# Forgetting attention on one Trainium2 core: the causal mask of diagonal blocks as a GpSimd select on the exponentials, in place of a third product in PSUM

## The chip, the cores and the metric

The kernel runs on one core of a Trainium2 chip. The core has five engines with queues of their own, each working strictly through its own program: TensorE (matmul; in the profile PE, and PEld for the loading of weights), VectorE (DVE), ScalarE (ACT), GpSimd (POOL) and SyncE (SP, which only issues transfers here). They wait for each other by semaphores. The metric is the device time of one execution in microseconds; of several runs the median counts.

## What is computed

One decoder layer with two groups of attention heads over a sequence of 2048. The edit is in the first group, forgetting attention: eight heads of width 64, causal, with a bias from cumulated log forget gates. Cut to what matters:

```python
def forgetting_attention(q, k, v, f_logit):
    cum = jnp.cumsum(jax.nn.log_sigmoid(f_logit.astype(jnp.float32)), axis=1)
    ...
    def one_block(args):
        qb, cb, n = args
        s = jnp.einsum('bhqd,bhkd->bhqk', qb, kh, preferred_element_type=jnp.float32) * scale
        s = s + cb[..., None] - cum[:, :, None, :]
        q_pos = n * Q_BLOCK + jnp.arange(Q_BLOCK)
        causal = key_pos[None, :] <= q_pos[:, None]
        s = jnp.where(causal, s, -jnp.inf)
        p = jax.nn.softmax(s, axis=-1)
        return jnp.einsum('bhqk,bhkd->bhqd', p.astype(vh.dtype), vh)
```

Around it: a normalised and modulated input, one input projection, a second group with a sliding window of 128 and sinks, SiLU gates, an output projection, a normalisation and the residual.

## The kernel before

The kernel works in float32 accuracy by splitting operands in a high and a low float16 part. It goes through three stretches: first setup, normalisation, projections and sliding-window attention; then the sweep of forgetting attention; then the output projection.

**The sweep.** It is a list of 160 steps, numbered from 0: eight heads of 20 steps. A head has four query chunks of 512 queries (`ci` = 0 to 3), and a chunk takes its key blocks of 128 in pairs, so 2, 4, 6 and 8 steps. Scores stand transposed: keys on the 128 partitions, queries along the row, at most 2 x 512 columns. The last two steps of a chunk hold the four diagonal blocks. There the columns of earlier queries are left out, so their widths are 512 + 384 = 896 and 256 + 128 = 384 columns instead of 1024. In a head these are the steps 0, 1, 4, 5, 10, 11, 18 and 19: 64 diagonal steps with 128 diagonal blocks in all.

**One step** has five parts, spread over its neighbours:

- `scores` (TensorE, line 1294 and 1295): per key block two products into the score tile `st` in PSUM (`sta` in the profile; there is only one such tile). The second product adds the cross terms, gate biases and row maxima. On a diagonal block a third (line 1297), an identity times `dmaskT`, adds -1e30 above the diagonal to the first 128 columns.
- `exp32` (ScalarE, line 1301): exponential of the tile to `p32`, float32, in SBUF (three buffers).
- `high` (ScalarE, line 1305): `p32` rounded to float16, the first half of `ph`.
- `low` (VectorE, line 1308): the rest, `p32` minus that half, to the second half of `ph`.
- `pv` (TensorE, lines 1318 to 1321): three small products for each 128 queries with the values.

The order of the work is written out by hand in the main loop. In step s, each engine's queue gets its share of this sequence: `exp32` of s; a `tick`, which releases delayed work such as the evacuation of projection tiles; `low` of s - 1; the first half of the step's filling work; `high` of s; `scores` of s + 1; a `tick`; `pv` of s - 2; the second half of the filling work. The filling work is projections of later heads (line 317) and products for row maxima of later chunks (line 1245, reduced by VectorE on lines 1248 and 1250).

So on ScalarE the copy `high` follows its exponential with only released evacuations between, and the exponential of the next step follows behind. On TensorE `scores` of s + 2 need the score tile that `exp32` of s + 1 reads out.

**GpSimd** does nothing in the sweep but issue transfers: gate tiles to memory (line 359, after VectorE's product on 357), weights (215), the maximum of a weight tile to memory and back (224, after VectorE's reduction on 221, and 229), and the output gate's weights (1176). In the setup it builds masks with `affine_select`, among them `dm32t` on line 514, which ScalarE turns into `dmaskT` (551); `identb` is a bfloat16 identity (458).

The row sum comes from a column of ones beside the values, so it holds what `ph` holds.

Of the kernel before, what the change touches and what calls it, by code (L numbers as in the profile page):

```python
# [10 lines left out]
F32 = mybir.dt.float32  # L11
F16 = mybir.dt.float16
BF16 = mybir.dt.bfloat16
I32 = mybir.dt.int32
AF = mybir.ActivationFunctionType
ALU = mybir.AluOpType
AX = mybir.AxisListType

P = 128
# [9 lines left out]
NEG = -1.0e30  # L29
# [4 lines left out]
XM, XR, VW = 66, 69, 129  # L34
# [7 lines left out]
def hybrid_layer(  # L42
# [17 lines left out]
    V, A, G, PE, SP = nc.vector, nc.scalar, nc.gpsimd, nc.tensor, nc.sync  # L60
# [12 lines left out]
    const = ctx.enter_context(tc.tile_pool(name="const", bufs=1))  # L73
# [73 lines left out]
    Shp = const.tile([P, KT], F32, name="Shp")  # L147

    ident = const.tile([P, P], F32, name="ident")
    identb = const.tile([P, P], BF16, name="identb")  # L150
    identh = const.tile([P, P], F16, name="identh")
    dmaskT = const.tile([P, P], BF16, name="dmaskT")
    lift = const.tile([P, 1], F32, name="lift")
    pfl = const.tile([P, 1], F32, name="pfl")
    csum = const.tile([P, 8, NB], F32, name="csum")
# [272 lines left out]
    start = ExitStack()  # L428
    st = start.enter_context(tc.tile_pool(name="start", bufs=1, reuse_waits="tile"))
    wad = start.enter_context(tc.tile_pool(name="wad", bufs=8, reuse_waits="tile"))  # L430
    with tc.manual_schedule():
# [23 lines left out]
            w_load(key, pieces(key))  # L455
        G.dma_start(snk[:], sinks[0].partition_broadcast(P))
        G.dma_start(bfg[:], b_fgate[0].partition_broadcast(P))
        V.tensor_copy(identb[:], ident[:])
        V.tensor_copy(identh[:], ident[:])
        PE.transpose(bk[0][:, :P], rows[:], ident[:])  # L460
        cols = st.tile([P, 40], F32, name="cols")
# [41 lines left out]
        zero = st.tile([P, 2 * P], F32, name="zero")  # L503
# [5 lines left out]
        dm32 = st.tile([P, P], F32, name="dm32")  # L509

        G.affine_select(dm32[:], zero[:, :P], [[-1, P]], ALU.is_ge, NEG, base=0, channel_multiplier=1)
        dm32t = st.tile([P, P], F32, name="dm32t")

        G.affine_select(dm32t[:], zero[:, :P], [[1, P]], ALU.is_ge, NEG, base=0, channel_multiplier=-1)

        G.affine_select(triu[:], ones[:], [[1, P]], ALU.is_ge, 0.0, base=0, channel_multiplier=-1)

        ang = st.tile([P, CH], F32, name="ang")
# [29 lines left out]
        A.activation(cs_[:], kh[:], AF.Sin)  # L548
        A.activation(sn_[:], sp_[:], AF.Copy, scale=-1.0)
        A.activation(dmask[:], dm32[:], AF.Copy)  # L550
        A.activation(dmaskT[:], dm32t[:], AF.Copy)

        def col8(name):
            return st.tile([P, KT], F32, name=name)
# [282 lines left out]
    class Pair:  # L837
# [9 lines left out]
        def scores(self):  # L847
            self.pss = ps_s.tile([P, 2, CH], F32, tag="s", name="pss")
            q = ab[self.j, self.i // 4]
            for e, (i, k0, nk) in enumerate(self.blocks):  # L850
                qo, o = (i % 4) * P, e * 2 * P
                for n, (a, b) in enumerate(((0, 0), (0, 1), (1, 0))):
                    for h in range(2):
                        r = slice(64 * h, 64 * h + 64)
                        PE.matmul(self.pss[:, h, o:o + nk * P], q[r, a, qo:qo + P],  # L855
                                  kst[self.g][r, b, k0 * P:(i + 1) * P], start=(n == 0), stop=(n == 2))
# [228 lines left out]
    with swa_order:  # L1085
# [10 lines left out]
        base = N_PRO  # L1096
# [179 lines left out]
    class Step:  # L1276
# [9 lines left out]
        def scores(self):  # L1286
            T, ci = Ts[self.hd % 2], self.ci
            self.st = ps_st.tile([P, 2 * CH], F32, tag="st", name="sta")
            for b, u0, o in self.blocks:
                w = CH - u0 * P  # L1290
                kb_ = slice(b * P, (b + 1) * P)
                qc = slice(ci * CH + u0 * P, (ci + 1) * CH)
                diag = b >= 4 * ci
                PE.matmul(self.st[:, o:o + w], T[:, 3, kb_], T[:, 1, qc], start=True, stop=False)  # L1294
                PE.matmul(self.st[:, o:o + w], T[0:XR, 2, kb_], T[0:XR, 0, qc], start=False, stop=not diag)  # L1295
                if diag:
                    PE.matmul(self.st[:, o:o + P], identb[:], dmaskT[:], start=False, stop=True)

        def exp32(self):
            self.p32 = fxp.tile([P, 2 * CH], F32, tag="p32", name="p32")  # L1300
            A.activation(self.p32[:, :self.w], self.st[:, :self.w], AF.Exp, scale=scl[f"qk{self.hd}"][:], bias=lift[:])  # L1301

        def high(self):
            self.ph = fxh.tile([P, 2, 2 * CH], F16, tag="ph", name="pha")
            A.activation(self.ph[:, 0, :self.w], self.p32[:, :self.w], AF.Copy)  # L1305
# [376 lines left out]
```

## Time and profile before

| | |
|---|---|
| median of 3 runs | 1194.2 us (1192.35 to 1195.01) |
| span of the profiled execution | 1188.7 us |
| TensorE busy in it | 1147.3 us (97%) |
| VectorE | 914.1 us (77%) |
| ScalarE | 665.9 us (56%) |
| GpSimd | 115.2 us (10%) |
| the sweep | about 480 to 1021 us |

The table's busy times are of one profiled execution; its span runs from its first to its last instruction. In rows of groups the columns are: line, engine, operation, output and inputs, shapes and count; then busy time in us and mean ns of one; then the engine's idle time just before, with what ended it. In rows in order of time the first number is the start in us, the second the duration, and brackets hold the idle time before it and its releaser. A row "A <- B" among the waits says how long A's engine stood idle until B was done: total, times, longest. Matmuls overlap in the array, so the time from one start to the next is their price, not their duration.

### The profile page before, as it was taken

What the parts mean: (1) busy time and instruction counts of PE and PEld (TensorE: products, weight loads), DVE (VectorE), ACT (ScalarE), POOL (GpSimd) and SP (SyncE); (2) the same over time, 40 slices, a digit from 0 to 9 for tenths busy, and PEclk for the clock granted to TensorE, in tenths of its full rate; (3) what the DMA queues carried; (4) which work ended last, traced back from release to release, by engine and by line L of the source; (5) the groups of instructions that cost most, each with busy time, mean ns of one, the idle gap of its engine ahead of it and who ended that gap; (6) DMA issues with size and microseconds to landing.
All of it is one profiled execution on the core that took longest, in us unless ns stands there. A gap on an engine that the chain in (4) does not pass through costs nothing.

```text
span 1188.7 us, 27244 instructions
## 1 busy us (share of the span) xinstructions
PE 1147.3 (97%) x10853; PEld 693.6 (58%) x10853; DVE 914.1 (77%) x2263; ACT 665.9 (56%) x1102; POOL 115.2 (10%) x231
## 2 busy tenths in 40 slices
PE   5899999999999998999999999999999999999997
PEld 2475556765558976555555555555555555555554
DVE  7876678687776748688888889887888887766665
ACT  2784345464655521476766667666666778433332
POOL 2000112212121211001000101001000000000000
PEclk9899999999999999999999999999999999999999
DMA  9745433314223322413325322212311345455642
GB/s 333 277 121 87 84 89 99 61 59 109 83 70 88 58 63 63 65 50 95 68 70 72 102 63 60 50 48 71 48 42 39 92 127 176 147 171 184 198 167 96
DMA packets 87579, 120.22 MB, mean 101 GB/s; under 512 B 27508, under 2 KB 63388, under 8 KB 87452
## 3 DMA queue, kind: packets, MB, share of 16 engines
q1 hardware_dynamic: 76184, 85.69, 24.4%
q0 software_dynamic: 10832, 32.50, 13.2%
q8 instruction: 85, 1.39, 0.6%
q14 instruction: 42, 0.34, 0.1%
q10 hardware_dynamic: 436, 0.28, 0.1%
HBM read 71.04 MB, written 25.18 MB: 81 GB/s over the span
## 4 chain that ended last, share of the span: by engine, by line
PE 79%; DVE 10%; DMA 6%; issue 2%; ACT 2%; SPq 1%; DVEq 0%; ACTq 0%
PE bk L317 29%; PE bk L1489 13%; PE bk L335 7%; PE sta L1295 4%; PE sta L1294 4%; PE bk L1245 4%; PE poa L1320 2%; PE poa L1321 2%; PE poa L1318 2%; DMA wa<-in_w_ada_dram 2%; PE pxb L888 2%; PE pss L855 2%; PE pob L907 2%; DVE a_m L1248 1%; PE bk L1410 1%
## 5 line engine op out<-in xcount | busy, mean ns | idle before, releaser
L1301 ACT ACTIVATE p<-sta,lift,scl_qk 128x1024 f32<-128x1024 f32 (+2 forms) x160 | 172.0, 1075 | 143.7 <-PE sta L1295 88.2
L317 PE MATMUL bk<-hT,wh_qk 128*128 128x512 f16 x768 | 195.3, 380 | 0.0
L1248 DVE TENSOR_REDUCE a_m<-bk 128x1 f32<-128x512 f32 x192 | 130.5, 686 | 55.2 <-PE bk L1245 54.0
L1308 DVE TENSOR_TENSOR pha<-p,pha 128x1024 f16<-128x1024 f32 (+2 forms) x160 | 169.1, 1057 | 0.2 <-ACT pha L1305 0.2
L1489 PE MATMUL bk<-wohl,oz 128*128 128x512 f16 x744 | 167.0, 379 | 0.7 <-DVE oz L1438 0.7
L1305 ACT ACTIVATE pha<-p 128x1024 f16<-128x1024 f32 (+2 forms) x160 | 148.1, 926 | 5.4 <-PE poa L1321 0.7
L1489 PEld LDWEIGHTS <-oz 128*128 128x128 f16 x744 | 71.9, 99 | 79.4 <-DVE oz L1438 2.8
L317 PEld LDWEIGHTS <-wh_qk 128*128 128x128 f16 x768 | 72.5, 98 | 78.2 <-issue 6.6
L1321 PE MATMUL poa<-vt,pha 128*128 128x65 f16 x1088 | 116.1, 192 | 1.4 <-DVE pha L1308 1.2
L1318 PE MATMUL poa<-vt,pha 128*128 128x65 f16 x1088 | 116.5, 193 | 0.5 <-DVE ona L1327 0.4
L1320 PE MATMUL poa<-vt,pha 128*128 128x64 f16 x1088 | 116.5, 194 | 0.0
L1245 PE MATMUL bk<-T 66*128 66x512 f16 (+2 forms) x320 | 110.2, 350 | 3.1 <-DVE a_m L1248 3.0
L1294 PE MATMUL sta<-T 128*128 128x512 f16 (+1 forms) x320 | 110.9, 346 | 2.5 <-ACT p L1301 2.4
L1318 PEld LDWEIGHTS <-pha 128*128 128x128 f16 x1088 | 101.5, 96 | 15.1 <-DVE ona L1327 1.5
L1295 PE MATMUL sta<-T 69*128 69x512 f16 (+1 forms) x320 | 109.8, 348 | 0.0
L1320 PEld LDWEIGHTS <-pha 128*128 128x128 f16 x1088 | 100.9, 97 | 11.4
L1321 PEld LDWEIGHTS <-pha 128*128 128x128 f16 x1088 | 100.8, 99 | 1.8 <-DVE pha L1308 1.7
L317 PE MATMUL bk<-hT,wh_za 128*128 128x512 f16 x384 | 99.7, 378 | 0.0
L335 PE MATMUL bk<-wh_va,hT 128*128 128x128 f16 x1536 | 90.7, 219 | 0.0
L335 PEld LDWEIGHTS <-hT 128*128 128x128 f16 x1536 | 87.5, 98 | 4.7 <-issue 2.1
L317 PE MATMUL bk<-hT,wh_zb 128*128 128x512 f16 x384 | 88.9, 379 | 0.0
L317 PE MATMUL bk<-hT,wh_qb 128*128 128x512 f16 x384 | 87.4, 379 | 0.0
(498 smaller groups left out, 1860.4 us busy)
## 6 DMA issues: line engine op xcount, KB each, us to landing
hT<-in_x_dram SPq DMA_DIRECT2D x20, 512.0 KB
wa<-in_w_ada_dram SPq DMA_DIRECT2D x16, 512.0 KB
z_d<-tz POOLq DMA_DIRECT2D x32, 256.0 KB, 2.9
T<-stq SPq DMA_DIRECT2D x64, 128.0 KB
T<-o_d SPq DMA_DIRECT2D x16, 512.0 KB
T<-z_d SPq DMA_DIRECT2D x16, 512.0 KB
out_dram<-hT SPq DMA_DIRECT2D x15, 512.0 KB
xt<-in_x_dram SPq DMA_DIRECT2D x12, 512.0 KB
```

The costliest lines, as they stand in the source:

```text
L317: PE.matmul(ps, whl[:, a, k, :], hT[ci][:, b, k, :], start=(k == 0 and n == 0), stop=(k == KT - 1 and n == 2))
L335: PE.matmul(ps[:, u * P:(u + 1) * P], hT[ci][:, a, k, u * P:(u + 1) * P], whl[:, b, k, :], start=(k == 0 and n == 0), stop=(k == KT - 1 an ...
L1245: PE.matmul(mx[:, :w], T[0:XM, 0, i * P:(i + 1) * P], T[0:XM, 2, pc * CH:pc * CH + w], start=True, stop=True)
L1294: PE.matmul(self.st[:, o:o + w], T[:, 3, kb_], T[:, 1, qc], start=True, stop=False)
L1295: PE.matmul(self.st[:, o:o + w], T[0:XR, 2, kb_], T[0:XR, 0, qc], start=False, stop=not diag)
L1301: A.activation(self.p32[:, :self.w], self.st[:, :self.w], AF.Exp, scale=scl[f"qk{self.hd}"][:], bias=lift[:])
L1305: A.activation(self.ph[:, 0, :self.w], self.p32[:, :self.w], AF.Copy)
L1308: V.tensor_tensor(self.ph[:, 1, :self.w], self.p32[:, :self.w], self.ph[:, 0, :self.w], op=ALU.subtract)
L1318: PE.matmul(po[:, u, :], ph[:, 0, pq], vt[:, b, hd, 0:65], start=(self.first and n == 0 and u == 0), stop=False)
L1320: PE.matmul(po[:, u, 0:64], ph[:, 0, pq], vt[:, b, hd, 65:VW], start=False, stop=False)
L1321: PE.matmul(po[:, u, :], ph[:, 1, pq], vt[:, b, hd, 0:65], start=False, stop=(self.last and n == len(self.blocks) - 1))
L1489: PE.matmul(py, self.hl[:, i, k, :], w_slot(8 * j + k)[:, cc], start=(k == 0 and m_ == 0), stop=(k == KT - 1 and m_ == 2))
```

## The change

The third product of the diagonal blocks goes, with the two constants that it reads. After the exponential of a diagonal step GpSimd sets to zero, in place in `p32`, what stands above the diagonal: the first 128 columns of each of the step's two blocks, which begin at column 0 and at `o1` (512 or 256). One instruction serves both; `[[0, 2], [1, P]]` counts the block with step 0 and the column with step 1, the partition with -1, so that a column is kept where query minus key is at least 0. `high` and `low` read `p32` after it.

```diff
-    identb = const.tile([P, P], BF16, name="identb")
...
-    dmaskT = const.tile([P, P], BF16, name="dmaskT")
...
-        V.tensor_copy(identb[:], ident[:])
...
-        dm32t = st.tile([P, P], F32, name="dm32t")
-
-        G.affine_select(dm32t[:], zero[:, :P], [[1, P]], ALU.is_ge, NEG, base=0, channel_multiplier=-1)
-
...
-        A.activation(dmaskT[:], dm32t[:], AF.Copy)
...
-                diag = b >= 4 * ci
                 PE.matmul(self.st[:, o:o + w], T[:, 3, kb_], T[:, 1, qc], start=True, stop=False)
-                PE.matmul(self.st[:, o:o + w], T[0:XR, 2, kb_], T[0:XR, 0, qc], start=False, stop=not diag)
-                if diag:
-                    PE.matmul(self.st[:, o:o + P], identb[:], dmaskT[:], start=False, stop=True)
+                PE.matmul(self.st[:, o:o + w], T[0:XR, 2, kb_], T[0:XR, 0, qc], start=False, stop=True)
 
         def exp32(self):
             self.p32 = fxp.tile([P, 2 * CH], F32, tag="p32", name="p32")
             A.activation(self.p32[:, :self.w], self.st[:, :self.w], AF.Exp, scale=scl[f"qk{self.hd}"][:], bias=lift[:])
+            if self.blocks[0][0] >= 4 * self.ci:
+
+                o1 = self.blocks[1][2]
+                dg = self.p32[:, :2 * o1].rearrange("p (b c) -> p b c", b=2)[:, :, 0:P]
+                G.affine_select(dg, dg, [[0, 2], [1, P]], ALU.is_ge, 0.0, base=0, channel_multiplier=-1)
```

## The prediction

> **What bounds the kernel now.** I read the page's head first, then the busy time by stretches, then who waited for whom, and at last single steps in order of time. The edit lies in the sweep of forgetting attention, which runs from about 480 to 1021 us.
>
> ```profile
> span 1188.7 us, 27244 instructions
> ...
> core 0: us, PE busy (x) PEld busy (x) DVE busy (x) ACT busy (x) POOL busy (x), PEclk, DMA share, GB/s
> 480.00:1021.00 541.00, 534.43 (x5496) 310.54 (x5495) 456.48 (x984) 372.88 (x440) 35.64 (x57) 1.00 0.32 73
> ```
>
> In this stretch TensorE is busy for 534.4 of 541 us at a granted clock of 1.00, VectorE for 456.5, ScalarE for 372.9, GpSimd for 35.6. A busy TensorE need not be a full one, since the ends of matmuls are modelled, so the waits are read beside it.
>
> ```profile
> PE sta L1294 <- ACT p L1301: 2.4, 5, 0.7
> PE bk L1245 <- DVE a_m L1248: 1.7, 4, 0.7
> ...
> ACT p L1301 <- PE sta L1295: 88.2, 74, 4.0
> ACT p L1301 <- PE sta L1297: 46.0, 41, 4.9
> ```
>
> Columns: waited in total, times, longest. In the whole sweep TensorE waited 2.4 us for the exponentials and 1.7 us for the maxima; the exponentials waited 134 us for TensorE (88.2 + 46.0). So TensorE sets the pace and ScalarE follows with slack. What shortens TensorE's stream here is worth its full length, until the slack of ScalarE is used up.
>
> **What is removed.** The third product of a diagonal block, line 1297.
>
> ```profile
> L1297 PE MATMUL sta<-dmaskT,identb 128*128 128x128 bf16 x128 | 26.5, 219 | 0.0
> ...
> 751.04 0.38 PE L1295 MATMUL sta<-T 69*128 69x512 f16 x1
> 751.26 0.22 PE L1297 MATMUL sta<-dmaskT,identb 128*128 128x128 bf16 x1
> 751.32 0.32 PE L1294 MATMUL sta<-T 128*128 128x384 f16 x1
> ...
> 751.65 0.22 PE L1297 MATMUL sta<-dmaskT,identb 128*128 128x128 bf16 x1
> 751.71 0.19 PE L1318 MATMUL poa<-vt,pha 128*128 128x65 f16 x1
> ```
>
> The first row gives the count, 128, and 26.5 us of busy time. That is not the price: 0.22 us is how long one is in flight, and the next product starts 0.06 us after it (751.26 to 751.32, 751.65 to 751.71). A quarter of the 512 columns that take 0.22 us from start to start (751.04 to 751.26) is 0.055. So 128 products give back 128 x 0.055 = 7.0 to 128 x 0.06 = 7.7 us; I take 7.4. Their weight loads run under other products and add nothing. The setup of the two constants goes away too: a cast and a select, of 0.23 and 0.29 us by the rows below, and a copy.
>
> ```profile
> L551 ACT ACTIVATE dmaskT<-dm32t 128x128 bf16<-128x128 f32 x1 | 0.3, 295 | 0.0
> ...
> PEld bk L479 <- DMA wa<-in_w_ada_dram: 6.0, 3, 4.1
> ```
>
> They stand in the first 20 us, on three engines, while TensorE's first products wait for weights from memory; I count them as nothing, and 0.3 us if that cover were gone.
>
> **What is added.** One GpSimd select in each of 64 diagonal steps (two per query chunk, four chunks, eight heads), on 2 x 128 columns in place. The trace has the operation in its setup, in the same size.
>
> ```profile
> 1.09 0.29 POOL masks.py:199 TENSOR_SCALAR_AFFINE_SELECT ident<-ident 128x128 f32<-128x128 f32 x1
> ...
> 1.41 0.23 DVE L458 CAST identb<-ident 128x128 bf16<-128x128 f32 x1 [0.19 <-POOL ident masks.py:199]
> ...
> 5.99 0.27 DVE L504 MEMSET zero<- 128x256 f32 x1
> ...
> 6.33 0.40 POOL L507 TENSOR_SCALAR_AFFINE_SELECT bm<-zero 128x256 f32<-128x256 f32 x1 [0.89 <-DVE zero L504]
> ```
>
> The select takes 0.40 us, starts 0.07 us after what it waited for (5.99 + 0.27 = 6.26 to 6.33), and a reader starts 0.03 us after its end (1.38 to 1.41). The new detour, from the end of the exponential to the earliest start of the float16 copy on line 1305, is so 0.5 us undisturbed; I use 0.6. The setup rows are selects on a quiet chip, so the other end stays open upwards and is priced below.
>
> Who waits for it: ScalarE, whose queue holds the copy and, behind it, the next step's exponential; behind that the scores of the step after next on TensorE, which need the score tile emptied. The row of an ordinary diagonal pair shows the cover.
>
> ```profile
> 500.22 1.10 ACT L1301 ACTIVATE p<-sta,lift,scl_qk 128x896 f32<-128x896 f32 x1 [1.72 <-PE sta L1297]
> 501.35 0.95 ACT L1305 ACTIVATE pha<-p 128x896 f16<-128x896 f32 x1
> 502.52 0.67 ACT L1301 ACTIVATE p<-sta,lift,scl_qk 128x384 f32<-128x384 f32 x1 [0.22 <-PE sta L1297]
> 503.31 0.52 ACT L1305 ACTIVATE pha<-p 128x384 f16<-128x384 f32 x1
> 505.70 1.20 ACT L1301 ACTIVATE p<-sta,lift,scl_qk 128x1024 f32<-128x1024 f32 x1 [1.86 <-PE sta L1295]
> ```
>
> Behind the wide copy ScalarE stood idle for 0.22 us, behind the narrow one for 1.86. A detour of 0.6 delays the second exponential (502.52 to 503.19) by about 0.4. Next on TensorE come the scores whose end released the third, at 505.70: four products of 0.22, so they began at about 504.7, and 0.4 late is still in time. The third isn't delayed at all. So an ordinary pair costs nothing; without that slack, 64 x 0.6 = 38 us would be the price.
>
> **GpSimd's queue.** The selects are put in among its DMA issues, in program order, and a select behind an issue that waits for VectorE starts late. This is the part that costs. Step 41 (second of head 2) in full:
>
> ```profile
> 625.88 0.67 ACT L1301 ACTIVATE p<-sta,lift,scl_qk 128x384 f32<-128x384 f32 x1 [1.61 <-PE sta L1297]
> 626.58 0.52 ACT L1305 ACTIVATE pha<-p 128x384 f16<-128x384 f32 x1
> 629.12 1.20 ACT L1301 ACTIVATE p<-sta,lift,scl_qk 128x1024 f32<-128x1024 f32 x1 [2.02 <-PE sta L1295]
> ...
> 627.51 0.57 POOL L224 DMA_DIRECT2D mx_d<-w_mx  x1 [21.98 <-DVE w_mx L221]
> 628.07 0.55 POOL L1176 DMA_DIRECT2D gw<-in_w_ada_dram  x1
> ...
> 628.06 1.08 DVE L1308 TENSOR_TENSOR pha<-p,pha 128x896 f16<-128x896 f32 x1
> ...
> 630.45 0.38 PE L1294 MATMUL sta<-T 128*128 128x512 f16 x1
> ```
>
> Both issues were put into the queue in step 40, ahead of the select of step 41. They are done at 628.62, so the copy starts at about 629.05 instead of 626.58 and ends at 629.6, the exponential of step 42 (629.12 to 630.32) ends 0.5 late, and the scores of step 43, which TensorE began at 630.45, are 0.3 to 0.4 us late. That is loss on the path.
>
> I did this for 62 diagonal steps (all but the last two, where no such scores follow): the copy starts at the later of exponential + detour and GpSimd's queue + 0.4, the ScalarE rows up to the next exponential are pushed, and what exceeds TensorE's start of the scores counts. With a detour of 0.6 the sum is 2.4 us, at five places: steps 20, 41, 81 and 145 behind an issue that waited for VectorE, and step 138 with 0.2. The first and the last of the four:
>
> ```profile
> 555.49 0.94 ACT L1305 ACTIVATE pha<-p 128x896 f16<-128x896 f32 x1
> ...
> 556.94 0.56 POOL L224 DMA_DIRECT2D mx_d<-w_mx  x1 [17.20 <-DVE w_mx L221]
> ...
> 970.24 0.52 ACT L1305 ACTIVATE pha<-p 128x384 f16<-128x384 f32 x1
> ...
> 971.39 0.54 POOL L359 DMA_DIRECT2D z_d<-tz  x1 [38.01 <-DVE tz L357]
> ```
>
> Each time GpSimd is free 1.7 to 2.0 us after the copy once began (557.5 against 555.49, 971.93 against 970.24). Longer detours sum to 2.9 us at 0.9, 3.7 at 1.2, 4.7 at 1.5, 6.8 at 1.8, 11.2 at 2.1 and 20.7 at 2.5: the slack gives way at about 1.8.
>
> The other way round, the issues behind a select now wait for that step's exponential, 1 to 3 us. They are loads of weights used many steps later and stores read after the sweep; GpSimd stood idle for 22 us ahead of the issue at 627.51. I count nothing.
>
> **VectorE.** Its subtraction of line 1308 reads the float32 tile and the copy, both in SBUF, and takes 1.08 us in the row above. If a select can't run beside it, a select that comes late into one waits for its rest: in step 41 from 628.62 to 629.14, which makes that loss 0.9 instead of 0.4. The trace shows no select in the sweep, so the bounds are 0 and a whole subtraction at every select, a detour of 0.6 + 1.08 to 1.2, about 1.8 us. I take a mean of 0.9, nearer to the free end, since in the pair at 500 us the selects would fall into stretches without one.
>
> The Trainium skill, SBUF — State Buffer, section "Who interferes with whom", speaks against the change here: a VectorE instruction with two SBUF inputs and a GpSimd instruction that reads SBUF hold a shared pair of ports in turn, and the second waits for the whole of the first. By that rule the bound of 1.8 is reached only where each select arrives just behind a subtraction; no run here shows it yet.
>
> **The sum.** -7.4 + 2.9 = -4.5 us. The profiled execution has a span of 1188.7, the median of the runs is 1194.2, 5.5 more outside the span; the edit touches nothing there. 1194.2 - 4.5 = 1189.7.
>
> **The rivals.**
>
> 1. Almost all of it is kept. TensorE's late starts after the four blocked steps are made up, because the few idle moments that it has now shrink: 7.4 us, 1186.8. For it: the losses are 0.4 to 0.8 us each. Against it: a stream that is 98.8% busy (534.4 of 541) has little to catch up with.
> 2. The gain is given back to the select. At a detour of 1.8 the loss is 6.8, the change -0.6: 1193.6. For it:
>
> ```profile
> L1308 DVE TENSOR_TENSOR pha<-p,pha 128x1024 f16<-128x1024 f32 (+2 forms) x159 | 168.5, 1060 | 0.2 <-ACT pha L1305 0.2
> ```
>
>    subtractions fill 168.5 of 541 us. Against it: the program puts the subtraction of the step before behind the exponential, and often it starts as the exponential ends. To the same result would lead VectorE, at 456.5 of 541 us, taking over as the bound; its 84 us of idle time speak against that.
> 3. Slower: ScalarE's queue becomes the bound at diagonal steps. Its place is the pair of diagonal steps, its price the loss above, its point of decision a detour of about 1.9 us, where the loss passes 7.4. At 2.1 it is 11.2, the change +3.8: 1198.0; at 2.5 it is +13.3. It needs selects that take three to four times their 0.40 us or a wait on VectorE for most of them. Against it: the setup rows; for it: none of them ran beside a busy VectorE.
>
> **How the numbers follow.** Forecast 0.50; rival 1 0.13; rival 2 0.20; rival 3 0.17. About 0.2%, 2.4 us, is what can be told from no change, so faster means below 1191.8 and slower above 1196.6. Forecast and rival 1 are faster, less a small part of the forecast that ends at 1192 (0.62 in all), rival 2 is the same (with that part 0.22), rival 3 slower (0.16, as some of it stays under 1196.6). The forecast's own range is 1187.5 to 1191.8. The range reaches from a full gain with the higher price per product (1194.2 - 7.7, less a little for the scatter of the runs) to rival 3 at its cheaper end: 1185.5 to 1198.5.
>
> **What would show it.** TensorE's products in the sweep should be 128 fewer and its stretch from the first to the last exponential shorter by 4 to 5 us. The waits should show the float16 copy waiting for the select, some 30 to 45 us in all over 64 steps, most of them 0.4 to 0.6; steps 20, 41, 81 and 145 should show 2 us or more, with GpSimd behind a DMA issue. The exponentials' wait for TensorE should fall by about as much. If selects last over 1 us, or start late although GpSimd's queue was empty and a subtraction is running, rival 2 or 3 is on its way. The prediction is wrong if TensorE's wait for the exponential rises from 2.4 to over 7 us, or if the stretch shortens by 7 us and GpSimd's queue never held a select.

## The result: no change in time

The changed kernel's median is 1193.49 us, the kernel before's on the same chip 1193.22, 20 runs each; the ratio is 1.0003, interval 0.9993 to 1.0012. A second measurement on another chip gave 0.9995 (0.9985 to 1.0005). Chips differ by a few us, so ratios are compared from here on; 0.001 is 1.2 us.

The page's head and the busy times of the sweep, after:

```profile
span 1189.9 us, 27084 instructions
...
PE 1142.1 (96%) x10725; PEld 687.0 (58%) x10725; DVE 916.0 (77%) x2262; ACT 663.8 (56%) x1101; POOL 147.5 (12%) x294
...
480.00:1021.00 541.00, 528.69 (x5356) 303.17 (x5355) 460.45 (x986) 371.21 (x440) 70.33 (x123) 1.00 0.32 74
```

The same line of the page before:

```profile
PE 1147.3 (97%) x10853; PEld 693.6 (58%) x10853; DVE 914.1 (77%) x2263; ACT 665.9 (56%) x1102; POOL 115.2 (10%) x231
```

On the whole page there are 128 matmuls fewer, as planned (10853 to 10725). TensorE is busy 5.7 us less between 480 and 1021 us (534.4 before). Yet the sweep isn't shorter: from the start of its first exponential to the end of its last it takes 537.2 us before and 538.7 after. So the products went and TensorE waits instead. The waits in the sweep, after (total, times, longest), and below them the row of before that the third answers to:

```profile
PE sta L1285 <- ACT p L1290: 6.5, 12, 1.0
PE bk L1237 <- DVE a_m L1240: 2.0, 4, 0.7
...
PEld L1286 <- issue: 9.5, 12, 1.2
...
ACT p L1290 <- PE sta L1286: 96.4, 96, 3.2
ACT pha L1299 <- POOL p L1295: 43.5, 52, 3.8
```

```profile
PEld L1295 <- issue: 3.8, 6, 0.8
```

TensorE's wait for the exponential went from 2.4 us in 5 places to 6.5 in 12, with the weight loads behind it (3.8 to 9.5; the same moments seen from the other queue). On ScalarE 38 us of waiting for TensorE (134 to 96) turned into 43.5 of the copy waiting for the select. To count TensorE's idle moments once, I took every pair of successive products from the start of the sweep's first exponential to the end of its last. What the second starts later than the shortest distance behind any product of the first's line and shape counts as idle, if it is over 15 ns: 9.7 us before, 17.3 after. The 7.6 us more are as much as the 7.4 that the products took. A second profile of the changed kernel shows 16.0 us; it lacks two gaps of 1.3 us in sum that the first has at 851.8 and 854.1 us. So 6.3 to 7.6 us were given back as idle time.

Where: five new gaps stand at the scores two steps behind a blocked select: 1.05 us behind step 20, 0.77 behind 41, 0.47 behind 61, 1.12 behind 81 and 0.76 behind 145, 4.2 us in sum. The second profile has them too, each within 0.01 us. Step 41 after the change, in order of time on ScalarE, GpSimd, VectorE and TensorE:

```profile
625.87 0.67 ACT L1290 ACTIVATE p<-sta,lift,scl_qk 128x384 f32<-128x384 f32 x1 [1.49 <-PE sta L1286]
629.55 0.52 ACT L1299 ACTIVATE pha<-p 128x384 f16<-128x384 f32 x1 [3.01 <-POOL p L1295]
629.98 1.19 ACT L1290 ACTIVATE p<-sta,lift,scl_qk 128x1024 f32<-128x1024 f32 x1
```

```profile
627.62 0.58 POOL L222 DMA_DIRECT2D mx_d<-w_mx  x1 [4.72 <-DVE w_mx L219]
628.20 0.55 POOL L1168 DMA_DIRECT2D gw<-in_w_ada_dram  x1
628.75 0.76 POOL L1295 TENSOR_SCALAR_AFFINE_SELECT p<-p 128x256 f32<-128x256 f32 x1
```

```profile
626.10 1.21 DVE L219 TENSOR_REDUCE w_mx<-wr_qk 128x1 f32<-128x1024 f32 x1
...
628.18 1.07 DVE L1302 TENSOR_TENSOR pha<-p,pha 128x896 f16<-128x896 f32 x1
```

```profile
631.22 0.38 PE L1285 MATMUL sta<-T 128*128 128x512 f16 x1 [0.61 <-ACT p L1290]
```

The exponential is done at 626.54. The select can't start before 628.75, since two issues stand ahead of it and the first waits for a reduction of VectorE (626.10 to 627.31). It then runs beside a subtraction and ends at 629.51 instead of 629.15; the subtraction ended at 629.25. The copy waits 3.0 us, the next exponential ends at 631.17, and the scores start at 631.22 after a wait.

### The profile page after: what moved, and what is told of

The parts are those of the page before. It is cut to its first block, busy times and chain, and to the rows that moved or that the text cites. A ratio compares the mean times of both kernels' runs of the same rounds, so it can differ in the third digit from the quotient of the medians.

```text
span 1189.9 us, 27084 instructions
## 1 busy us (share of the span) xinstructions
PE 1142.1 (96%) x10725; PEld 687.0 (58%) x10725; DVE 916.0 (77%) x2262; ACT 663.8 (56%) x1101; POOL 147.5 (12%) x294
## 4 chain that ended last, share of the span: by engine, by line
PE 75%; DVE 12%; DMA 5%; issue 3%; ACT 2%; SPq 1%; POOL 0%; DVEq 0%; ACTq 0%; POOLq 0%
PE bk L315 27%; PE bk L1483 13%; PE bk L333 7%; PE sta L1286 4%; PE sta L1285 4%; PE bk L1237 4%; DMA wa<-in_w_ada_dram 2%; PE poa L1315 2%; PE poa L1314 2%; PE poa L1312 2%; PE pxb L880 2%; PE pss L847 2%; DVE a_m L1240 2%; PE pob L899 2%; DVE pha L1302 1%
## 5 line engine op out<-in xcount | busy, mean ns | idle before, releaser
L1299 ACT ACTIVATE pha<-p 128x1024 f16<-128x1024 f32 (+2 forms) x160 | 148.2, 926 | 51.2 <-POOL p L1295 43.5
```

## The experiments

Three theories. Theory A, the queue: the gain is real, and most of it is lost where a select stands behind an issue that waits for VectorE. The port theory: it is lost because a select and a two-input instruction of VectorE exclude each other. Theory C: the products' time was never worth anything. All runs are compared with the kernel before on the same chip, and every ratio has its interval behind it.

**Neither product nor select.**

```diff
-                G.affine_select(dg, dg, [[0, 2], [1, P]], ALU.is_ge, 0.0, base=0, channel_multiplier=-1)
...
+            if self.blocks[0][0] >= 4 * self.ci:
+                A.activation(self.p32[:, :self.w], self.st[:, :self.w], AF.Identity, scale=0.0, bias=lift[:])
+            else:
+                A.activation(..., AF.Exp, ...)
```

> The changed kernel without its select, so neither product nor select; the mask of the diagonal blocks is left out, and the exponential of the 64 diagonal steps is replaced by a ScalarE Identity with scale 0 that writes a constant (same shapes, same buffers). Theory A (the 128 products gave back 7.4 us and the selects took them again): 7.4 us under the kernel before, ratio 0.994, TensorE's idle moments in the sweep about as before. Theory C (the products' time was never on the path, so the selects cost nothing either): ratio 0.998 to 1.000.

Measured: 0.9951 (0.9938 to 0.9963), 5.8 us faster; the sweep takes 531.6 us. TensorE's idle moments are 11.1 us, 1.4 more than before, and 7.4 - 1.4 = 6.0 agrees with the time. Theory C falls. The 1.4 us are idle time that comes with a faster TensorE even where no select exists. The Identity is 0.09 us shorter than the exponential whose place it takes (1.01 against 1.10 us at 896 columns), which may flatter this run a little.

**Both.**

```diff
             A.activation(self.p32[:, :self.w], self.st[:, :self.w], AF.Exp, ...)
+            if self.blocks[0][0] >= 4 * self.ci:
+                ...
+                G.affine_select(dg, dg, [[0, 2], [1, P]], ALU.is_ge, 0.0, base=0, channel_multiplier=-1)
```

> The kernel before, its third product kept, with the select added behind the exponential of the diagonal steps. Theory A: the select alone costs what took the gain away, 6 to 8 us over the kernel before, ratio 1.005 to 1.007. Theory C: nothing, 1.000.

Measured: 1.0018 (1.0009 to 1.0027), 2.1 us slower, a third of what was expected. TensorE's idle moments rose by 3.7 us, 3.4 of them at the same five places. So the two edits don't add up: with the products the select costs 2.1 us, without them 5 to 6 (1.0003 and 0.9995 against 0.9951). The products had probably been part of what hid it.

**GpSimd's issues moved to SyncE, with the change and without it.**

```diff
+    dq = [G]
...
-        G.dma_start(md[:], mx[:])
+        dq[0].dma_start(md[:], mx[:])
...
     with tc.manual_schedule():
         mi = 0
+        dq[0] = SP
```

The other four issues of the sweep are edited in the same way.

> The changed kernel with the transfers that GpSimd issues in the sweep (gate tiles, weights, weight maxima, output gate) issued by SyncE instead, so that a select has nothing ahead of it that waits for VectorE. Queue theory: the loss at the starts of heads and at step 145 goes, 4 to 5.5 us under the kernel before, ratio 0.9955, and no select starts more than 0.2 us after its exponential except beside a subtraction. Port theory (what costs is that selects and VectorE's two-input instructions exclude each other): the loss stays, ratio 0.999 to 1.000, with as many selects of 0.7 to 1.2 us as now.

> The kernel before with the same transfers issued by SyncE: what the move is worth by itself. Both theories: ratio 1.000, within 0.002; if it isn't, the difference has to be taken off the run before.

Measured: 0.9987 (0.9976 to 0.9997) with the change, 1.0033 (1.0022 to 1.0043) without it. The move alone costs 3.9 us, which neither theory had expected; the two against each other give 0.9954, 5.5 us in favour of the select. The five gaps are gone in the first, and no select starts more than 0.13 us after its exponential. That is what theory A forecast, once the price of the move is taken off; the ratio by itself, 0.9987, lies between the two theories, and 7 selects still last over 0.65 us. SyncE is the wrong place: its queue also carries the stores of queries and keys that TensorE waits for. The weight loads' waits of the kernel before with the move show it:

```profile
PEld L1247 <- DMA T<-stq: 2.5, 1, 2.5
```

**The issues left to GpSimd, but one step later**, with the change and without it. They are kept in a list and put into the queue behind the next step's exponential, so behind its select:

```diff
+    def later(f):
+        pend.append(f) if sweep else f()
...
-        G.dma_start(md[:], mx[:])
+        later(lambda: G.dma_start(md[:], mx[:]))
...
             stp_.exp32()
+            while pend:
+                pend.pop(0)()
             tick()
```

> The changed kernel, transfers still issued by GpSimd, but in the sweep the gate stores, the weight maxima (both ways) and the output gate's loads are put into its queue one step later, behind the next step's select. Queue theory: no select starts more than 0.2 us after its exponential, TensorE's idle moments in the sweep fall from 17.2 to 12 or 13 us, 4 to 5 us under the kernel before, ratio 0.9955 to 0.997. Port theory: the selects that last 0.7 us and more stay, and with them the time, ratio 0.999 to 1.000.

> The kernel before with the same issues put one step later: what the move is worth by itself. Both theories: ratio 1.000, within 0.002, since nothing of the sweep waits for these transfers.

Measured: 0.9967 (0.9956 to 0.9978) with the change, 0.9998 (0.9986 to 1.0009) without it. The order alone is worth nothing. With the select it is worth 4.3 us against the ratio of the result and 3.3 against that of the second measurement. Step 41 of the first, on GpSimd and ScalarE:

```profile
625.03 0.41 POOL L1303 TENSOR_SCALAR_AFFINE_SELECT p<-p 128x256 f32<-128x256 f32 x1 [3.71 <-ACT p L1298]
626.04 0.59 POOL L227 DMA_DIRECT2D mx_d<-w_mx  x1 [0.60 <-DVE w_mx L224]
626.62 0.55 POOL L1176 DMA_DIRECT2D gw<-in_w_ada_dram  x1
```

```profile
624.29 0.67 ACT L1298 ACTIVATE p<-sta,lift,scl_qk 128x384 f32<-128x384 f32 x1 [1.49 <-PE sta L1294]
625.47 0.52 ACT L1307 ACTIVATE pha<-p 128x384 f16<-128x384 f32 x1 [0.51 <-POOL p L1303]
```

The same three entries of the queue in another order: the select starts 0.07 us after its exponential, and the copy waits 0.51 us instead of 3.01. All five gaps are gone; TensorE's idle moments fall to 13.8 us, more than the 12 to 13 expected, and its wait for the exponential to 2.9:

```profile
PE sta L1293 <- ACT p L1298: 2.9, 6, 0.7
```

Of the 13.8 us some 1.4 aren't waits: products between 948.9 and 952.3 us took twice their time, at a granted clock of 0.50.

**A memset for the select**, in the deferred kernel and in the changed one.

```diff
-                G.affine_select(dg, dg, [[0, 2], [1, P]], ALU.is_ge, 0.0, base=0, channel_multiplier=-1)
+                G.memset(dg, 1.0)
```

> As the first of these, with each select replaced by a GpSimd memset of the same 2 x 128 columns, which writes and doesn't read; the diagonal blocks are set to one, so the mask is left out. Port theory: none of them lasts over 0.5 us beside a subtraction, and the run is 1.5 to 3 us faster than the one with selects. If reading isn't the cause, some memsets last 0.7 us and more just as the selects do, and the two runs agree within 1 us.

> The changed kernel with its queue as it is, each select replaced by a memset of the same columns (diagonal blocks set to one, so the mask is left out): the queue's waits without the subtraction's. If the two add up, TensorE's idle moments behind steps 20, 41, 61, 81 and 145 fall from 4.2 us in sum to 2 to 2.5, what the walk through the rows of before gave for the queue alone, and the time lies between the changed kernel and the one with issues put later, ratio 0.998. If the queue alone costs the 4.2 us, they stay.

Both leave the mask out. Measured: 0.9958 (0.9942 to 0.9974) deferred, 0.9963 (0.9952 to 0.9975) undeferred. The instruction's own rows (duration in ns: least, median, longest), of the changed kernel and of the deferred memset:

```profile
L1295 POOL TENSOR_SCALAR_AFFINE_SELECT p<-p x64: 396/406/1207, 482.2 to 1019.9; 128x256 f32<-128x256 f32 x64
```

```profile
L1303 POOL MEMSET p<- x64: 311/311/330, 482.6 to 1014.3; 128x256 f32 x64
```

Of 64 selects 12 last 0.7 us or more. Eleven of those overlap a subtraction of line 1302 that had started ahead of them, the twelfth another VectorE instruction with two inputs in SBUF (line 1432); no memset lasts over 0.33, beside the same subtractions. The Trainium skill, SBUF — State Buffer, section "Who interferes with whom", says that a VectorE instruction with two SBUF inputs contends with a GpSimd instruction that reads SBUF and not with one that only writes it, and that their shared ports are an exclusive lock; these rows agree. Step 5 of the changed kernel shows a wait for the whole rest of a subtraction, first GpSimd's row and then VectorE's:

```profile
503.59 0.97 POOL L1295 TENSOR_SCALAR_AFFINE_SELECT p<-p 128x256 f32<-128x256 f32 x1 [1.61 <-ACT p L1290]
```

```profile
503.08 1.22 DVE L1302 TENSOR_TENSOR pha<-p,pha 128x1024 f16<-128x1024 f32 x1
```

The subtraction ends at 504.30, the select 0.26 later, at 504.56. In time the deferred memset and the deferred select can't be told apart (0.9958 and 0.9967, 1.1 us, overlapping intervals), so 1.5 to 3 us isn't shown. TensorE's idle moments are 11.7 us, 2.1 fewer, but 1.4 of these are the half clock in the profile of the select.

In the undeferred one the five gaps fall from 4.2 to 2.2 us, inside the 2 to 2.5 expected: 0.92 and 0.63 are left behind steps 20 and 145, 0.30 and 0.31 behind 41 and 81, none behind 61. So about half of that loss is the queue alone, and most of the other half comes from selects that leave the queue into a subtraction; a memset is also 0.09 us shorter than an undisturbed select. The time missed its expectation of 0.998. On one chip the memset in the old order took 3.8 us off the changed kernel (0.9963 against 0.9995), and the new order with selects 2.1 (0.9977, below). Which of the two remedies is worth more isn't settled, since their intervals overlap. Either one takes back a good part, and together they give little more than the memset alone, 0.9958: steps 41, 61 and 81 need both a late select and a subtraction. So the queue isn't the only cause; the selects held up by subtractions are another, of about the same worth.

**The subtraction moved behind the copy**, in the deferred kernel.

```diff
             stp_.exp32()
...
-            if s:
-                steps[s - 1].low()
...
             stp_.high()
+            if s:
+                steps[s - 1].low()
```

> The changed kernel with its issues one step later, and in addition VectorE's subtraction of the step before put behind the float16 copy instead of behind the exponential. Port theory: other selects, and fewer (under 6 instead of 8), last over 0.7 us, and the time is equal or up to 1 us better than that of the issues put later alone. If it gets slower by over 1 us, the subtraction's place matters for what waits for VectorE, and the old place is better.

Measured: 0.9998 (0.9986 to 1.0011), the gain gone. 13 selects instead of 8 last over 0.65 us, against the expectation, and the small products now wait for the subtraction, as the waits show, here first and in the deferred kernel below it:

```profile
PE poa L1323 <- DVE pha L1310: 4.6, 5, 1.8
```

```profile
PE poa L1323 <- DVE pha L1310: 0.8, 2, 0.6
```

Not all of the loss is waiting. From 949.2 to 956.0 us TensorE's granted clock was 0.50, and over the whole execution the mean of its runs is 0.9903, against 0.9917 in the deferred kernel on the same chip. 0.0014 of 1190 us is an estimated 1.7 us, of 2.5 between the two ratios (0.9998 and 0.9977).

**Once more on one chip**, the changed kernel and the deferred one.

> The changed kernel as it is, beside the others on one chip. Ratio 0.999 to 1.002.

> The changed kernel with its issues one step later, as run once already, beside the unaltered changed kernel on one chip: queue theory 3.5 to 5 us under it, ratio to the kernel before 0.996 to 0.997.

Measured: 0.9995 (0.9985 to 1.0005) and 0.9977 (0.9968 to 0.9987): 2.1 us between them, less than expected, and the intervals just touch. The idle moments are 16.0 and 14.0 us, of the latter some 1.5 at half clock. The deferred kernel is the best of those that compute the whole layer: two ratios to the kernel before, both clear of 1.

## Why the prediction was right or wrong

*What bounds the kernel.* Right. Taking work from TensorE alone made it 5.8 us faster, and most of the 38 us of slack that ScalarE lost to the select cost TensorE nothing.

*What is removed.* 7.4 us was the right price of the products; what it was worth was 5.8 (4.4 to 7.4), since a faster TensorE waits 1.4 us more for others even without a select. The prediction counted the full length.

*What is added.* The detour of an undisturbed select is 0.51 to 0.58 us in the trace, against 0.5 read from the setup and 0.6 used. At the undisturbed steps no new gap of the size of the five stands behind it, as forecast.

*GpSimd's queue.* The mechanism and the places were right: steps 20, 41, 81 and 145, to which 61 came, and 138 with a small gap. The copy waited for selects 43.5 us in sum, inside the 30 to 45 named.

*The step that failed is the sum*: -4.5 us was forecast, none came, and the sweep, forecast to be 4 to 5 us shorter, wasn't. Its larger error is the term 2.9 us for the select, which measured 5 to 6 in time (1.0003 and 0.9995 against 0.9951); the smaller is the 7.4, worth 5.8. The 2.9 was the walk's value for a mean detour of 0.9, spread over all steps alike. But late selects aren't spread. VectorE is late at these places; the instruction that it is late with frees the queue, and at three of the five its work just after is a subtraction, which then holds the select up again. At 41, 61 and 81 the selects lasted 0.76, 1.10 and 1.10 us. The prediction had worked this out for step 41 (0.9 us instead of 0.4; 0.77 was measured) and then averaged it away. Of the 6.3 to 7.6 us of added idle time, 4.2 stand at the five places and 1.4 are those of the run without products and selects; the rest, 0.7 to 2.0, is scattered over later steps. Part of it is selects beside VectorE's two-input instructions: the scores two steps behind 138, where the prediction's walk had 0.2 us, wait 0.33 us, and those behind 151 wait 0.66. With a memset in place of the select, in either order, the first gap is gone and the second is 0.39; before the change they were 0 and 0.21. The remainder wasn't isolated.

The prediction's own sign of being wrong, TensorE's wait for the exponential above 7 us, just failed to show at 6.5; it was set too high, as 4.1 us more of that wait and what else came with it were enough to undo the gain. And its 5.5 us outside the span are a misreading that the sum survived: an execution is 1.7 us longer than its span (1191.62 and 1189.9 after), and most of the rest must be the difference between a quick execution and the median.

So the time was that of rival 2, the gain given back to the select, and not by rival 2's way, which was a long detour at every diagonal step: 52 of 64 selects lasted under 0.7 us. That the time lies in the wide range of the prediction is owed to the rivals in it, not to the forecast.

That the select's cost rises as the products go (2.1 to 5 or 6 us) is shown; that the products' time in TensorE's queue is what covered it is the reading that fits, argued from the rows and not tried by itself.

## What to carry to other kernels

An engine that only issues transfers looks idle, and its queue isn't: an instruction put there starts behind every issue that still waits. Before work moves to it, list per step what stands ahead of it and put waiting issues behind it; here the same entries in another order made no change into 0.2 to 0.3% faster. Ask also what the instruction will run beside: here an instruction that only writes did as well in the old order as a reading one in the new. And where two causes of delay come from the same late engine, price them together at the places where it is late, not as a mean over all steps.

## What was not expected of the hardware

After the 2.5 us wait of the kernel before with its issues on SyncE, TensorE ran at half its clock for 3.4 us. The busy times by stretches of that run; the number behind the engines' is the granted clock:

```profile
497.00:501.00 4.00, 1.92 (x22) 1.07 (x20) 3.35 (x12) 1.51 (x3) 0.00 (x0) 1.00 0.97 244
501.30:504.70 3.40, 3.40 (x20) 1.52 (x17) 1.44 (x3) 0.82 (x2) 0.00 (x0) 0.51 0.48 117
505.00:510.00 5.00, 5.00 (x64) 3.03 (x63) 2.38 (x9) 4.03 (x5) 0.00 (x0) 1.00 0.10 11
```

The wait stands in the first row, at a clock of 1.00; the stretch behind it was granted 0.51, and three products of 512 columns took 1.47 us there instead of 0.81, as the rows below show. One wait was so paid for twice, which is part of the 3.9 us that the move cost. The runs bear it out: their mean granted clock is 0.9911, against 0.9929 in the kernel before on that chip, and 0.0018 of 1190 us is an estimated 2.1 us.

```profile
501.53 1.47 PE L319 MATMUL bk<-hT,wh_za 128*128 128x512 f16 x3
```

The same at full clock, in the kernel before:

```profile
600.77 0.81 PE L317 MATMUL bk<-hT,wh_qk 128*128 128x512 f16 x3
```

It doesn't take a wait of this length. In the two profiles of the deferred kernel such a stretch begins at 948.9 and at 948.6 us, behind 3.4 us in which TensorE was busy for 63% and no gap was over 0.7 us. The changed kernel was busy for only 56% of the 3.4 us from 621.2 us and kept its full clock. What decides between the two isn't shown here.
